# Moving the gate row and the context products later in a fused diffusion layer's projection stage

## The chip, the cores and the metric

The kernel runs on one core of a Trainium2 chip. The metric is the device time of one execution in microseconds (us). A core has a matrix engine (PE, TensorE), three elementwise engines (ACT, ScalarE; DVE, VectorE; POOL, GpSimd) and SP (SyncE), which here does nothing but issue DMA transfers. Each engine carries out its own instructions in order and meets the others through semaphores.

## The reference

One layer on 1024 latent tokens (a 16 by 64 grid) and 256 context tokens, model width 1024, float32. What the change touches is the modulated input, its projection and the gate:

```python
def hybrid_layer(x, ctx, c, c_ctx, w_ada, b_ada, norm_g, w_in, ...):
    shift, scale, gate = adaln(c, w_ada, b_ada)        # silu(c) @ w_ada + b_ada, in three
    shift_c, scale_c, gate_c = adaln(c_ctx, w_ada, b_ada)
    h = rmsnorm(x, norm_g) * (1 + scale[:, None]) + shift[:, None]
    hc = rmsnorm(ctx, norm_g) * (1 + scale_c) + shift_c
    q, k, v, za, u, bg, cg, zc = jnp.split(h @ w_in, SPLIT_POINTS, axis=-1)
    q = rmsnorm(heads(q), q_norm_g)
    k = rmsnorm(heads(k), k_norm_g)
    kc, vc = jnp.split(hc @ w_in[:, D_ATTN:3 * D_ATTN], 2, axis=-1)
    kc = rmsnorm(heads(kc), k_norm_g)
    attn = neighbourhood_attention(q, k, heads(v), kc, vc, rpb) * jax.nn.silu(za)
    conv = gated_short_conv(u, bg, cg, zc, conv_w, conv_b)
    return x + gate[:, None] * (jnp.concatenate([attn, conv], axis=-1) @ w_out)
```

`hc` is what the kernel calls the context's factors; `hc @ w_in[...]` are the context's products; `gate` is the gate row.

## The kernel before, in words

**Four stages.** A first stage (`STEPS`) works out shift and scale, writes the modulated latent input `h`, and already projects the first conv group's three column blocks with it. Its PSUM banks are six accumulators `acc..` and two banks `tr`, in which, among others, the adaLN products lie. Then comes the projection stage, to which the change belongs, then attention (with the remaining projections as filler work for PE), then the output projection.

**The projection stage.** The loop at L1151 runs over steps n = 0 to 34. The 32 token tiles are four head pairs (p = n // 8) by eight tiles of 128 tokens (t = n % 8). In step n, PE projects tile n to q, k and v of pair p (`proj_tile`, L304): 24 matmuls, three for each of eight chunks of 128 rows of the weights, because float32 products are made of a high and a low part. The rest of a tile's work follows in later steps: in step n + 1 ACT squares it and DVE sums (`head_scale`), POOL takes the power -0.5, ACT saves v (`put_v`); in step n + 2 ACT scales it (`rms_normed`: the last read of the tile's bank), and DVE rotates it (`rotated`); at the end of step n + 4, n even, PE transposes tiles n and n + 1 (`turn_qk`), and one step on ACT and DVE split the result and SP stores it. Step t = 4 to 7 of a pair also splits one chunk each of the next pair's weights on ACT and DVE (`chunk_split`), and step t = 0 of the next pair splits the last four, just ahead of its own tile.

**What sets the order.** `strict` (L553) chains the instructions of every engine, SP's transfers included, in the order in which the program writes them. So no engine can pass over an instruction that waits. A PSUM tile of a tag gets its bank when all instructions that touch the tag's earlier tile in that bank are done, those that the program writes further down too. The tags in this stage are O and S (two banks each, tiles `pacc`), U (two banks: `cacc`, `pu`, `pgate`) and C (two banks, transposes).

**The context.** `CONTEXT` (L42) writes the factors `hc` in pairs: DVE scales (`hw`), ACT adds the shift (high part), DVE takes the low part. It is done in step 0 (L1189-1190). In step t = `at` of each pair (L1155: 2, 2, 2, 0), PE makes the context's products of that pair in both U banks (`ctx_products`, L1234); in step `at` + 1 `ctx_sums` and `head_scale` add and square them on ACT and DVE; in step `at` + 2 `normed_ctx` reads them a last time on ACT; in step `at` + 3 `turn_kc` transposes the keys.

**The first conv group.** In steps 5 to 8 PE makes two ticks (six matmuls each) of the projection to the gate path z (`next(group0)`, L1194-1196). Its result lies in tiles `pu` of tag U: one for the first half of the tokens, taken in step 5, one for the second, taken in step 7. The weights for it, `uraw`, are loaded in step 0; ACT casts them to the high parts `uh` at the end of step 0 (`do_acts`, L1228), DVE takes the low parts `ul` in step 1 (`do_dves`).

**The gate row.** `gate.load` (steps 1 to 8) has SP load the 4 MB of its weights in blocks of 512 KB; `gate.add` (steps 2 to 9) multiplies a block and adds it on DVE; `gate.split` (step 11), `gate.sum` (step 13, four matmuls in U banks `pgate`) and a transfer in step 16 (L1175) bring the row to where the output stage needs it. Steps 8, 9, 13, 14, 18, 19, 23 and 24 also add blocks of `w_out` on DVE (`add_blocks`).

Of the kernel before, what the change touches and what calls it, by code (L numbers as in the profile page):

```python
# [23 lines left out]
KT = D // P  # L24
# [3 lines left out]
NPAIR = NH // 2  # L28
# [21 lines left out]
CONTEXT = "Hi0 Hi1 Lo0 Lo1 Hi2 Hi3 Lo2 Lo3 Hi4 Hi5 Lo4 Lo5 Hi6 Hi7 Lo6 Lo7"  # L50
# [5 lines left out]
def body(tc, es, x, xb, xt, cb_, ct, w_mod, w_gate, b_ada, w_grp, w_col, q_g, k_g, bias, w_out, vecs, cst, out):  # L56
# [31 lines left out]
    def mm3(ps, ah, al, bh, bl, first, last):  # L88

        i = pe.matmul(ps, ah, bh, start=first, stop=False)  # L90
        pe.matmul(ps, ah, bl, start=False, stop=False)
        pe.matmul(ps, al, bh, start=False, stop=last)
        return i
# [79 lines left out]
    def chunk_load(col, k):  # L173
        raw = wpp.tile([P, 3, P], F32, name="wr", tag="wr", bufs=5)
        sp.dma_start(raw[:].rearrange("p a n -> p (a n)"), w_grp[NPAIR if col == CU else (col - CQ) // P, k])
        return raw

    def chunk_split(raw):
        raw = raw[:].rearrange("p a b -> p (a b)")
        w = wpp.tile([P, 2, 384], F32R, name="w", tag="w", bufs=12)  # L180
        wh, wl = w[:, 0], w[:, 1]
        act.copy(wh, raw)
        dve.tensor_tensor(wl, raw, wh.bitcast(F32), ALU.subtract)
        return wh, wl, w[:, :, P:384]
# [4 lines left out]
    def head_scale(pp, ps, n):  # L189

        act.activation(sq[:, :n, :HD], by_head(ps[:, :n * HD]), AF.Square, scale=0.125)
        ss = pp.tile([P, 4], F32, name="ss", tag="ss", bufs=7)
        dve.tensor_reduce(ss[:, :n], sq[:, :n], AX.X, ALU.add)
        pool.tensor_tensor(ss[:, :n], ss[:, :n], mhalf[:, :n], ALU.pow)
        return ss
# [10 lines left out]
    def next_vs():  # L206
        vss.append(vss.pop(0))
        return vss[-1]

    def spill_v(p, b, vs):  # L210
        spill(v_d[p][:, :, b:b + 2].rearrange("p s b d -> p s (b d)"), vs.rearrange("p s i d -> p s (i d)"))

    def put_v(vs, i, ps):

        act.copy(vs[:, :, i], ps.rearrange("p (s d) -> p s d", s=2))

    def normed(qn, ps, scale, n):
        for h in range(n):
            cols = slice(h * HD, (h + 1) * HD)
            act.activation(qn[:, cols], ps[:, cols], AF.Identity, scale=scale[:, h:h + 1])  # L220
# [6 lines left out]
    def rms_normed(pp, ps, scale):  # L227

        qn = pp.tile([P, 256], F32, name="qn", tag="qn", bufs=3)
        normed(qn, ps, scale, 4)  # L230
        return qn

    def rotated(pp, rope, qn, t):

        rot = pp.tile([P, 256], F32, name="rot", tag="rot", bufs=3)
        tmp = pp.tile([P, 256], F32, name="rtmp", tag="rtmp", bufs=1)
        for i, to in enumerate((rot, tmp)):
            dve.tensor_tensor(to[:].rearrange("p (k h d) -> p k h d", k=2, h=2),
                              qn[:].rearrange("p (k h d) -> p k h d", k=2, h=2),
                              rope[:, i, t].rearrange("p k (o d) -> p k o d", o=1).broadcast_to([P, 2, 2, HD]),  # L240
                              ALU.mult)
        r4, t4 = (v[:].rearrange("p (h f i) -> p h f i", h=8, f=2) for v in (rot, tmp))
        for f in range(2):
            dve.tensor_tensor(r4[:, :, f], r4[:, :, f], t4[:, :, 1 - f], ALU.add)
        return qn, rot
# [33 lines left out]
    def ctx_sums(pp, acc):  # L279
        for a in acc:  # L280
            other = pp.tile([P, 256], F32, name="rtmp", tag="rtmp")
            act.copy(other, a[:, 256:])
            dve.tensor_tensor(a[:, :256], a[:, :256], other, ALU.add)
# [21 lines left out]
        return put  # L305

    def proj_tile(ch, t):
        ps = bank("pacc", "OOSS"[t % 4])
        for k in range(KT):
            wh, wl = ch[k][:2]  # L310
            mm3(ps[:, :384], hh[k][:, t * P:(t + 1) * P], hl[k][:, t * P:(t + 1) * P], wh, wl, k == 0, k == KT - 1)
        return ps


    def unit_load(col):
        raws = []
        for q in range(2):
            raws.append(uw.tile([P, 4, P], F32, name="uraw", tag="uraw", bufs=2))
            sp.dma_start(raws[q], w_col[col // P, :, 4 * q:4 * q + 4])
        return raws  # L320
# [85 lines left out]
    def z_col(f):  # L406
        return CZA + f * P if f < 4 else CZC + (f - 4) * P
# [342 lines left out]
    def do(steps):  # L750
        for word in steps.split():
            name = word.rstrip("0123456789")
            at = word[len(name):]
            does[name](*([int(at)] if name in ("warm", "fill") else map(int, at)))
# [37 lines left out]
    def bank(name, tag):  # L792
        return (pss if tag == "S" else psm).tile([P, 512], F32, name=name, tag=tag, bufs=2)
# [329 lines left out]
    gate = gate_row()  # L1123
# [5 lines left out]
    def load_blocks(i):  # L1129

        for fs in K_HALVES:
            wsum.append(bmp.tile([P, 3 * 384], F32, name="ws", tag="bt", bufs=2)[:, :D])
            sp.dma_start(wsum[-1], w_out[0, fs[i] * P:(fs[i] + 1) * P])
# [13 lines left out]
    def flush():  # L1147
        while stores:
            stores.pop(0)()

    for n in range(NT + 3):  # L1151


        p, t = divmod(n, NB)
        at = 2 if p < NPAIR - 1 else 0  # L1155
        if t and p + 1 < NPAIR:
            raws.append(chunk_load(CQ + (p + 1) * P, t))
        if n == 0:
            loaded[z_col(4)] = unit_load(z_col(4))
        if n == NT - 8:  # L1160
            loaded[z_col(0)] = unit_load(z_col(0))
        if 1 <= n <= KT:
            gate.load(n - 1)
        if n == NT - 3:
            act.activation(few[:, 5:6], ones, AF.Exp)
        if n == NT - 6:
            heads[0].masks()
            heads[0].load_k()
        if n == NT - 5:
            heads[0].load_q()  # L1170
        flush()
        blocks = divmod(n - 6, 5)
        if 6 <= n < 26 and blocks[1] == 0:
            load_blocks(blocks[0])
        if n == 16:  # L1175
            sp.dma_start(ab[:, :, 0], g_d.rearrange("o (t p) -> p (o t)", p=P))

        if t == 0 and 0 < n < NT:
            nxt += map(chunk_split, raws)
            ch, nxt, raws = nxt, [], []  # L1180
        if t == 0 and p + 1 < NPAIR:
            raws.append(chunk_load(CQ + (p + 1) * P, 0))
        if n == 0:
            next(group0)
        if n == NT - 4:
            next(fill)
        if n < NT:
            tiles[n] = proj_tile(ch, t)
            if n == 0:  # L1189
                do(CONTEXT)  # L1190
        else:
            for _ in range((4, 3, 1)[n - NT]):
                next(fill)
        if 5 <= n < 9:  # L1194
            for _ in range(2):
                next(group0)
        if n == 9:
            for _ in group0:
                pass
        if 0 < n <= NT:  # L1200
            scales[n - 1] = head_scale(pp, tiles[n - 1], 4)
            if n % 2:
                vs = next_vs()
            put_v(vs, (n - 1) % 2, tiles[n - 1][:, 256:384])
            if n % 2 == 0:
                q, r = divmod(n - 1, NB)
                spill_v(q, r - 1, vs)
        if t == at + 1 and n < NT:
            ctx_sums(pp, cacc)
            cscales = [head_scale(pp, a, 2) for a in cacc]  # L1210

        if 1 < n <= NT + 1:
            m, r = n - 2, (n - 2) % NB
            qn = rms_normed(pp, tiles[m], scales.pop(m))
        while waiting:
            waiting.pop(0)()
        if 4 <= t and p + 1 < NPAIR:
            nxt.append(chunk_split(raws.pop(0)))
        if 1 < n <= NT + 1:
            tiles[m] = rotated(pp, rope, qn, r)  # L1220
        if t == at + 2 and n < NT:
            kc = normed_ctx(pp, cacc, cscales)
        do_dves()
        if 6 <= n < 26 and blocks[1] in (2, 3):
            add_blocks(*blocks)
        if 2 <= n < KT + 2:
            gate.add(n - 2)
        do_acts()  # L1228

        if n == KT + 3:  # L1230
            gate.split()
        if n == KT + 5:
            gate.sum()
        if t == at and n < NT:  # L1234
            cacc = ctx_products(ch)
        if n % 2 == 0 and n >= 4:
            waiting.append(turn_qk(pp, (n - 4) // NB, [tiles.pop(n - 4), tiles.pop(n - 3)], (n - 4) % NB))
        if t == at + 3 and n < NT:
            waiting.append(turn_kc(pp, p, *kc))
# [74 lines left out]
    with sbuf("att") as ap, psum("psb") as psb:  # L1314
# [6 lines left out]
        for n in range(len(TICKS)):  # L1321
# [11 lines left out]
            if ready:  # L1333
                p = ready.pop()
# [266 lines left out]
```

## Time and profile before

| what | us |
|---|---|
| median of 3 runs | 588.11 |
| the runs | 587.42 to 588.27 |
| the profiled execution's own time | 587.34 |
| its span, first to last instruction | 585.6 |
| PE busy in the span | 577.2 (99%) |
| DVE busy | 438.6 (75%) |
| ACT busy | 282.0 (48%) |
| POOL busy | 57.4 (10%) |

The span begins with the first instruction. The projection stage's first tile starts on PE at 63.00 us, its last ends at about 241 us. In rows of a timeline, the first two figures are the start and the duration in us; neighbouring instructions of a kind are merged, with their number behind an x; what stands in square brackets is the time for which the engine was idle before, and what ended it. An instruction can start on ACT or DVE while the one before it is still in its last stages, so what counts in a chain is the distance from start to start. The mean granted clock of PE in this execution is 0.999.

### The profile page before, as it was taken

How to read it: one execution, taken by the hardware profiler on the slowest of the kernel's cores; microseconds unless marked ns; L12 is line 12 of the kernel's file. 1: busy time of each engine (PE TensorE's matmuls, PEld its weight loads, DVE VectorE, ACT ScalarE, POOL GpSimd, SP SyncE). 2: the span in 40 equal slices, each digit the busy share in tenths (PEclk: the TensorE clock that was granted, in tenths of full speed). 3: DMA queues.
4: the chain of work that ended last, by engine and by line, in shares of the span. 5: the costliest groups of instructions: out<-in, count | busy, mean ns of one | idle time of the engine just before them, and what ended most of it. 6: DMA issues, size and time to landing. Idle time of an engine off the chain costs nothing.

```text
span 585.6 us, 9903 instructions
## 1 busy us (share of the span) xinstructions
PE 577.2 (99%) x3531; PEld 483.3 (83%) x3532; DVE 438.6 (75%) x890; ACT 282.0 (48%) x653; POOL 57.4 (10%) x82
## 2 busy tenths in 40 slices
PE   8899999999999999999999999999999999999997
PEld 4578999999999999988878787878787867888886
DVE  1578879656846746367998788998979887999952
ACT  5636355336525545433463474466535646643420
POOL 1001033123223232100000000000000001100000
PEclk9999999999999999999999999999999999999999
DMA  8997666845756695686253646564758273773532
GB/s 323 410 415 278 220 229 211 283 166 194 267 189 213 224 341 205 226 297 219 73 209 120 243 140 229 182 216 155 254 187 257 80 263 96 248 252 89 199 125 91
DMA packets 66679, 126.14 MB, mean 215 GB/s; under 512 B 8714, under 2 KB 27650, under 8 KB 64325
## 3 DMA queue, kind: packets, MB, share of 16 engines
q1 hardware_dynamic: 66244, 124.70, 60.8%
q0 software_dynamic: 384, 0.81, 0.6%
q8 instruction: 28, 0.46, 0.3%
q14 instruction: 23, 0.18, 0.1%
HBM read 92.38 MB, written 33.10 MB: 214 GB/s over the span
## 4 chain that ended last, share of the span: by engine, by line
PE 91%; DMA 5%; DVE 2%; ACT 1%; SPq 0%; issue 0%; POOL 0%; DVEq 0%; ACTq 0%
PE pu L71 29%; PE pacc L71 23%; PE pout L71 13%; PE acc L71 5%; PE po L71 5%; PE cacc L71 4%; PE pss L71 3%; DMA xn<-in_xb 3%; PE pc L71 3%; PE pmx L71 2%; PE trA L71 1%; PE tr L71 1%; DMA y_d<-tb 1%; PE ptot L71 1%; PE trB L71 1%; DVE sb L71 0%
## 5 line engine op out<-in xcount | busy, mean ns | idle before, releaser
L71 PE MATMUL pu<-h,uh 128*128 128x512 f32 x544 | 174.4, 402 | 0.0
L71 PE MATMUL pacc<-w,h 128*128 128x384 f32 x768 | 138.5, 337 | 0.0
L71 PEld LDWEIGHTS pacc<-w,h 128*128 128x128 f32 x768 | 132.8, 188 | 0.2
L71 PEld LDWEIGHTS pu<-h,uh 128*128 128x128 f32 x544 | 97.3, 188 | 18.4 <-issue 1.2
L71 PE MATMUL pu<-h,ul 128*128 128x512 f32 x272 | 106.5, 391 | 0.0
L71 PE MATMUL pout<-right,left 128*128 128x512 f32 (+2 forms) x348 | 77.0, 383 | 0.0
L71 PEld LDWEIGHTS pout<-right,left 128*128 128x128 f32 x348 | 64.4, 188 | 12.7
L71 PEld LDWEIGHTS pu<-h,ul 128*128 128x128 f32 x272 | 51.1, 188 | 11.5
L71 POOL TENSOR_TENSOR ss<-ss,few 128x4 f32<-128x4 f32 (+1 forms) x40 | 41.4, 1035 | 127.0 <-DVE ss L71 126.7
L71 ACT COPY sc<-pc 128x512 f32<-128x512 f32 x32 | 18.7, 587 | 44.6 <-PE pc L71 44.6
L71 PE MATMUL acc<-h,w 128*128 128x512 f32 x144 | 35.3, 397 | 1.4 <-ACT h L71 1.4
L71 ACT ACTIVATE sc<-sc 128x512 f32<-128x512 f32 x32 | 20.3, 633 | 33.7 <-DVE sc L71 33.6
L71 ACT ACTIVATE sq<-pacc 128x256 f32<-128x256 f32 x32 | 12.3, 386 | 47.4 <-PE pacc L71 46.7
L71 DVE TENSOR_TENSOR sum<-sum,sb 128x372 f32<-128x372 f32 (+2 forms) x64 | 31.1, 485 | 2.7
L71 PEld LDWEIGHTS acc<-h,w 128*128 128x128 f32 x144 | 26.3, 188 | 7.8 <-ACT h L71 2.1
L71 DVE SCALAR_TENSOR_TENSOR m<-pout,ab,m 128x512 f32<-128x512 f32 (+2 forms) x34 | 22.9, 717 | 13.0 <-PE pout L71 12.9
L71 ACT ACTIVATE qn<-pacc,ss 128x64 f32<-128x64 f32 x128 | 30.0, 330 | 4.8 <-PE trA L71 2.5
L71 DVE TENSOR_TENSOR mx<-mx,sb 128x372 f32<-128x372 f32 (+2 forms) x64 | 30.8, 481 | 1.4
L71 DVE TENSOR_REDUCE ss<-sq 128x4 f32<-128x260 f32 (+1 forms) x40 | 15.7, 393 | 21.5 <-ACT sq L71 21.5
L71 DVE TENSOR_TENSOR ul<-uraw,uh 128x512 fp32r<-128x512 f32 x34 | 23.1, 685 | 10.0 <-ACT uh L71 10.0
L71 DVE TENSOR_TENSOR sb<-pss,bt 128x192 f32<-128x192 f32 (+3 forms) x48 | 27.5, 600 | 2.3 <-PE pss L71 2.2
L71 DVE TENSOR_TENSOR qs<-trA,qs 128x512 fp32r<-128x512 f32 x16 | 11.1, 691 | 21.2 <-ACT qs L71 20.2
(142 smaller groups left out, 862.8 us busy)
## 6 DMA issues: line engine op xcount, KB each, us to landing
uraw<-in_w_col SPq DMA_DIRECT2D x34, 256.0 KB, 3.8
slab<-in_w_mod SPq DMA_DIRECT2D x8, 1024.0 KB, 9.0
q_d<-qs SPq DMA_DIRECT2D x32, 256.0 KB, 4.0
k_s<-k_d SPq DMA_DIRECT2D x8, 1024.0 KB, 6.9
q_s<-q_d SPq DMA_DIRECT2D x16, 512.0 KB, 3.9
wr<-in_w_grp SPq DMA_DIRECT2D x40, 192.0 KB, 5.0
bt<-in_rpb SPq DMA_DIRECT2D x8, 564.0 KB, 6.8
xn<-in_xb SPq DMA_DIRECT2D x8, 512.0 KB
```

What stands on the lines that cost most here:

```text
L71: i = emit(*a, **kw)
```

## The change

Four edits in the projection stage. The gate row's loads, additions, split, sum and last transfer each come eight steps later. The context's factors are written in step 2, after tile 0 is scaled, and no longer in step 0 right behind tile 0's matmuls. The context's products of pair 0 come in step 4 and no longer in step 2 (the other pairs' stay; a fifth entry of the tuple serves the steps beyond the last tile). The tiles with t % 4 of 0 and 1 take the S banks, where the first stage's `tr` tiles lay, and those of 2 and 3 the O banks. Steps 5 to 8 of the first conv group are as they were.

```diff
     def proj_tile(ch, t):
-        ps = bank("pacc", "OOSS"[t % 4])
+        ps = bank("pacc", "SSOO"[t % 4])
...
         p, t = divmod(n, NB)
-        at = 2 if p < NPAIR - 1 else 0
+        at = (4, 2, 2, 0, 0)[p]
...
-        if 1 <= n <= KT:
-            gate.load(n - 1)
+        if 9 <= n <= KT + 8:
+            gate.load(n - 9)
...
-        if n == 16:
+        if n == 24:
             sp.dma_start(ab[:, :, 0], g_d.rearrange("o (t p) -> p (o t)", p=P))
...
             tiles[n] = proj_tile(ch, t)
-            if n == 0:
-                do(CONTEXT)
...
             qn = rms_normed(pp, tiles[m], scales.pop(m))
+        if n == 2:
+            do(CONTEXT)
         while waiting:
             waiting.pop(0)()
...
-        if 2 <= n < KT + 2:
-            gate.add(n - 2)
+        if 10 <= n < KT + 10:
+            gate.add(n - 10)
         do_acts()
 
-        if n == KT + 3:
+        if n == KT + 11:
             gate.split()
-        if n == KT + 5:
+        if n == KT + 13:
             gate.sum()
```

## The prediction, made before the change was run

> **What bounds the kernel now.** I read the busy times first, then the stage that the change touches by windows, then the timelines of PE, ACT and DVE in it. The first view is the table of windows; its columns are the busy time of PE, of PE's weight loads, of DVE, ACT and POOL, then the granted clock.
>
> ```profile
> 63.00:253.00 190.00, 190.00 (x1100) 182.12 (x1099) 125.71 (x304) 89.72 (x318) 46.68 (x51) 1.00 0.68 234
> ```
>
> In the whole projection stage PE is busy for 190.00 of 190.00 us at full clock. So there is no wait of PE that this change could take away, and whatever wait it adds there is added to the end. PE's timeline shows how the stage starts:
>
> ```profile
> 63.00 12.67 PE L71 MATMUL pacc<-w,h 128*128 128x384 f32 x72
> 75.50 5.71 PE L71 MATMUL cacc<-w,hc 128*128 128x512 f32 x32
> 81.05 8.48 PE L71 MATMUL pacc<-w,h 128*128 128x384 f32 x48
> ...
> 89.94 4.43 PE L71 MATMUL pacc<-w,h 128*128 128x384 f32 x24
> 94.22 0.63 PE L71 MATMUL pu<-h,uh 128*128 128x512 f32 x2
> ```
>
> Three tiles take 75.50 - 63.00 = 12.50 us, so 4.17 each; the context's products take 81.05 - 75.50 = 5.55; between tile 4's end at 81.05 + 8.33 = 89.38 and 89.94 stand six transposes, 0.56; tile 5 takes 4.28; then the conv group takes its first `pu` bank.
>
> **The change, part by part: who holds the U banks in step 5.** With `at` = 4, PE does tiles 0 to 4 (63.00 + 5 x 4.17 = 83.85), the products (to 89.40), the transposes (89.96) and tile 5 (94.24), and then comes `pu`, as before the change. But the products now hold both U banks, and their last reader is `normed_ctx`, in step `at` + 2 = 6. In ACT's order that stands behind the squaring of tile 5, which PE finishes only at 94.24. So PE must wait at `pu`, and behind `pu` everything of PE is queued. Before, step `at` + 2 was step 4, and the banks were free in time. This wait is certain in the code; its length is ACT's and DVE's backlog. To lay that out I need the rows of the stage's start, of SP, then DVE and POOL, then ACT:
>
> ```profile
> 70.80 0.82 SPq L71 DMA_DIRECT2D uraw<-in_w_col  x2
> ```
> ```profile
> uraw<-in_w_col SPq DMA_DIRECT2D x34, 256.0 KB, 3.8
> ```
> ```profile
> 70.47 0.87 DVE L71 SCALAR_TENSOR_TENSOR hw<-xc,ab,rs 128x256 f32<-128x256 f32 x2
> ...
> 77.10 0.88 DVE L71 SCALAR_TENSOR_TENSOR hc<-hw,ab,hc 128x256 fp32r<-128x256 f32 x2 [0.18 <-ACT hc L71]
> 78.88 0.42 DVE L71 TENSOR_REDUCE ss<-sq 128x4 f32<-128x260 f32 x1 [0.89 <-ACT sq L71]
> 79.22 1.28 DVE L71 TENSOR_TENSOR ul<-uraw,uh 128x512 fp32r<-128x512 f32 x2
> ```
> ```profile
> 81.79 0.42 DVE L71 TENSOR_TENSOR rot<-qn,rope 128x256 f32<-128x256 f32 x1 [0.95 <-ACT qn L71]
> ...
> 83.00 1.41 DVE L71 SCALAR_TENSOR_TENSOR gacc<-gs,c,gacc 128x512 f32<-128x512 f32 x2
> ```
> ```profile
> 79.38 1.41 POOL L71 TENSOR_TENSOR ss<-ss,few 128x4 f32<-128x4 f32 x1 [8.95 <-DVE ss L71]
> ```
> ```profile
> 77.38 1.13 ACT L71 CAST uh<-uraw 128x512 fp32r<-128x512 f32 x2
> 78.41 0.37 ACT L71 ACTIVATE sq<-pacc 128x256 f32<-128x256 f32 x1
> ...
> 80.83 0.93 ACT L71 ACTIVATE qn<-pacc,ss 128x64 f32<-128x64 f32 x4 [0.89 <-POOL ss L71]
> ```
>
> Before, the factors (7.51 us, from 70.47 to 77.98 on DVE) ran while `uraw` was on its way, and the cast of `uraw` found its data there. Now the cast is what ACT comes to first, right behind the first stage, and the factors are behind it in step 2. SP issues `uraw` at 70.80 and about 71.2 as before (nothing ahead of it moves); with the median of 3.8 us it lands at 75.0 or, behind the rope table issued just before it, later. I take 75.8 for the second half; the ends are 75.0 and 77.4, where the cast stood without a wait. So ACT, and with it DVE, stands idle until 75.8 while tiles 0 to 2 are already done. From there:
>
> Tile 0 is squared at 76.3 (half of 1.13 on), its sum is there at 77.1 (0.37 + 0.42), its power at 78.1 to 78.5 (POOL has 1.03 to 1.41), and ACT has scaled it at about 79.3. DVE does the sum, `ul` and the sum of tile 1 (0.33 + 1.20 + 0.33 from 76.7) to 78.6, then the factors, 7.5, to 86.2. Then rotation of tile 0 (81.79 to 83.00: 1.2), sum of tile 2 (0.33), rotation of tile 1 (1.2), sum of tile 3 (0.33): 89.3. There it waits for ACT's first chunk cast, which stands behind the scaling of tile 2 (sum at 87.8, power 1.0, scaling 0.8, cast 0.55: 90.2), then low part of the chunk 0.5, rotation of tile 2 1.2, sum of tile 4 0.33: at 92.3 DVE comes to the first of the two context sums, which PE had ready at 89.4. From the second copy of a sum on, the same work stands in ACT's rows of pair 1:
>
> ```profile
> 134.03 0.37 ACT L71 COPY rtmp<-cacc 128x256 f32<-128x256 f32 x1 [0.56 <-PE trA L71]
> ...
> 136.78 1.20 ACT L71 CAST gp<-gacc 128x512 fp32r<-128x512 f32 x2
> 138.29 0.38 ACT L71 ACTIVATE sq<-pacc 128x256 f32<-128x256 f32 x1 [0.32 <-PE pacc L71]
> ...
> 139.51 0.55 ACT L71 CAST w<-wr 128x384 fp32r<-128x384 f32 x1
> 139.91 0.57 ACT L71 ACTIVATE kn<-cacc,ss 128x64 f32<-128x64 f32 x2
> 140.32 0.32 ACT L71 COPY vs<-cacc 128x128 f32<-128x128 f32 x1
> ```
>
> The second copy starts at 92.3 + 0.43 (a sum of this width, like the 0.42 of the rotation's) + 0.05 = 92.8. To the end of the transposes' casts it is 136.78 - 134.03 = 2.75; `gp` isn't there in step 5 now, but a chunk cast is (0.40); tile 5's squaring to the chunk cast of step 6 is 139.51 - 138.29 = 1.22; from there to the release of the first bank 140.64 - 139.51 = 1.13. Together 92.8 + 5.5 = 98.3. PE waits from 94.2 to 98.3: **4.1 us**. Bounds: were ACT not behind at all, only tile 5's squaring to the release would follow PE (0.2 + 2.35, so 2.6); with `uraw` at 77.4 it is 1.6 more, 5.7.
>
> **The gate row.** Its additions leave steps 2 to 9, where DVE's time was hidden, and where DVE's backlog above is already counted without them. They come in steps 10 to 17, a pair of 1.33 us each (83.00, 1.41 long, less the overlap). In steps 10 and 11 DVE idles for the context's products and takes them up; in 11 `gate.split` (1.2 us) goes as well; from step 12 on they add up until step 16, in which the last four weight chunks of pair 2 must be split just ahead of tile 16. DVE's rows of steps 13 to 16, and PE's:
>
> ```profile
> 144.33 0.69 DVE L71 TENSOR_TENSOR qs<-trA,qs 128x512 fp32r<-128x512 f32 x1 [0.96 <-ACT qs L71]
> ...
> 146.93 1.41 DVE L71 TENSOR_TENSOR ws<-ws 128x512 f32<-128x512 f32 x2
> ...
> 150.31 0.42 DVE L71 TENSOR_TENSOR ks<-trC,ks 128x256 fp32r<-128x256 f32 x1 [0.70 <-ACT ks L71]
> ...
> 152.40 1.41 DVE L71 TENSOR_TENSOR ws<-ws 128x512 f32<-128x512 f32 x2
> ...
> 154.51 0.69 DVE L71 TENSOR_TENSOR qs<-trA,qs 128x512 fp32r<-128x512 f32 x1 [0.36 <-ACT qs L71]
> ...
> 157.11 1.96 DVE L71 TENSOR_TENSOR w<-wr,w 128x384 fp32r<-128x384 f32 x4
> ```
> ```profile
> 147.10 1.09 PE L71 MATMUL pgate<-gp,oner 128*1 128x512 f32 x4
> 148.03 0.38 PE L71 MATMUL trC<-ci,kn 128*128 128x128 f32 x2
> ...
> 153.01 8.60 PE L71 MATMUL pacc<-w,h 128*128 128x384 f32 x48
> ```
>
> All in before's times: step 13 starts its transposes' part at 144.33 and ends its `w_out` part at 148.26; with the pair 149.6. Step 14: sum 0.33, then 150.31 to 153.73 (3.42), pair: 154.7. Step 15: sum 0.33, 154.51 to 157.11 (2.60), pair: 158.9. The first of the four chunks is split 0.55 later, at 159.45. PE comes to tile 16 at 153.01 + 4.27 = 157.28, less the 0.93 of `pgate`, which now is in step 21: 156.35; it needs that chunk's low part at its fourteenth matmul, 13 x 0.174 later, at 158.6. Wait: **0.8 us**; the further chunks (0.49 each) keep ahead of PE (0.52 each). Before, the slack there was 1.9. Ends: 0, if DVE keeps up, and 2.1, if step 12's pair isn't absorbed either. The eight loads move on SP past the chunk loads and stores of pair 1; each waits for a buffer that DVE frees two steps ahead of its use; a late one would lengthen the 0.8, within its upper end. `pgate` costs PE its 0.93 in either place; step 24's transfer has nobody waiting until the output stage.
>
> **Parts that cost nothing.** The S banks' last reader is ACT's copy of the context's row, the last of twelve `tr` tiles and so in the second bank:
>
> ```profile
> 63.30 0.38 ACT L71 COPY rs<-tr 128x256 f32<-128x256 f32 x1
> ```
>
> It is done at 63.7, and the bank is needed for tile 1 at 67.17; were it the first bank, 0.7. Tile 4 needs tile 0's bank at 79.68, tile 0 is scaled at 79.3: hidden by 0.4, up to 1.0 if `uraw` is late. The factors' last pair is there at 86.2, and PE comes to it at 83.85 + 6 x 0.69 = 88.0. The transposes at 89.4 need tile 1 rotated at 89.0.
>
> **The sum.** 4.1 + 0.8 = 4.9. Against the profiled execution's own time 587.34 + 4.9 = 592.2; the median of the runs lies 0.77 above that execution, so 593.0 is what I give.
>
> **Rivals.** One: the wait lets PE's clock fall. The rows of PE's start price that:
>
> ```profile
> 1.52 2.74 PE L71 MATMUL acc<-warm 128*128 128x512 bf16 x6 [1.52 <-POOL warm L71]
> ...
> 4.48 3.20 PE L71 MATMUL acc<-warm 128*128 128x512 bf16 x14
> ```
> ```profile
> PE acc L71 <- POOL warm L71: 1.5, 1, 1.5
> ```
>
> The same matmul takes 2.74 / 6 = 0.46 us first and 3.20 / 14 = 0.23 later: for about 2.9 us PE ran at half rate and lost some 1.4. Losing that once or twice behind the wait gives 594.4 to 595.8, middle 595.1. Against it: 4.1 us is short, but the longest wait in PE's whole list is the 1.5 us at the very start, so nothing in this trace shows either way; I give it 0.20. [...]
>
> Two, not slower: `pu` finds a U bank in time. The place is step 5, and the point is whether ACT's last read of the first context accumulator ends before 94.2. Then only the gate row's 0.8 is left: 588.9, within what can be told from no change. For it: before the change the banks were never waited for. Against it: the program order puts the read behind tile 5's end. 0.12.
>
> Three, faster: DVE's relief in steps 2 to 9 and the earlier squaring of tile 0 pay. Against it: PE's 190.00 of 190.00; nothing there can be won, and more than 1.2 us would be needed. 0.03. A last 0.03 is for further waits behind a late `uraw`, above 596.
>
> **How the numbers follow.** My forecast has 0.62; with its bounds alone it spans 588.11 + 2.6 = 590.7 to 588.11 + 7.8 = 595.9. The range 590.6 to 596.0 leaves out rival two, rival three and the last case, 0.18. About 0.2% (1.2 us) is what a measurement of this kernel can tell from no change: faster 0.03, same 0.12, slower 0.85.
>
> **What would show it.** Right: PE's waits name `pu` <- ACT `vs` (or `kn`) with about 4 us near 94, and `pacc` <- DVE `w` with about 0.8 us at tile 16 near 161 to 163; ACT idles some 10 us ahead of `uh`, for `uraw`; all else on PE is shifted by the sum. Wrong: PE without a gap at 94, a gap at another step of the first eight, matmuls of 0.35 us behind the gap (rival one), or a sum of PE's gaps that isn't the difference of the times.

## The result and the profile after

The changed kernel takes 596.13 us (median of 4 runs: 595.63, 595.74, 596.52, 599.0) beside 587.87 us for the kernel before on the same chip (4 runs, 587.42 to 588.27). The ratio is 1.0156, with a 95% interval of 1.0142 to 1.0169: slower. (Ratios here are worked out from the executions of both kernels, not from the two medians, whose quotient is 1.0141.) The forecast was 593.0 with 590.6 to 596.0 around it, so the direction is right and the time lies 0.13 us above the range. The profiled execution took 595.63 us with a span of 593.9, beside 587.34 and 585.6 before: 8.3 us more in both. One execution of e9 below, which took 1488.66 us, was a disturbed one and is left out of its ratio.

PE's list of waits in the changed kernel (columns: total, times, longest, all in us) has three entries of the projection stage that the list before did not have:

```profile
PE pu L71 <- ACT vs L71: 4.5, 1, 4.5
...
PE pacc L71 <- DVE w L71: 1.1, 1, 1.1
...
PE pacc L71 <- ACT qn L71: 0.2, 1, 0.2
```

The first two are the waits that the prediction named, at the places that it named. PE's timeline shows them with what stands around them:

```profile
80.29 4.45 PE L71 MATMUL pacc<-w,h 128*128 128x384 f32 x24 [0.24 <-ACT qn L71]
84.58 5.71 PE L71 MATMUL cacc<-w,hc 128*128 128x512 f32 x32
...
90.70 4.44 PE L71 MATMUL pacc<-w,h 128*128 128x384 f32 x24
99.66 0.73 PE L71 MATMUL pu<-h,uh 128*128 128x512 f32 x2 [4.52 <-ACT vs L71]
...
100.58 1.05 PE L71 MATMUL pu<-h,uh 128*128 128x512 f32 x2
101.43 0.63 PE L71 MATMUL pu<-h,ul 128*128 128x512 f32 x1
101.86 1.05 PE L71 MATMUL pu<-h,uh 128*128 128x512 f32 x2
...
159.80 6.08 PE L71 MATMUL pacc<-w,h 128*128 128x384 f32 x34
166.98 2.21 PE L71 MATMUL pacc<-w,h 128*128 128x384 f32 x11 [1.09 <-DVE w L71]
```

Tile 5 ends at 90.70 + 4.44 = 95.14, and `pu` starts 4.52 us later. Look then at the `pu` rows behind the wait: from the pair at 100.58 to the single product at 101.43 it is 0.85 us, so 0.43 for each matmul, and from the single to the next pair another 0.43. At full clock the same matmul takes 0.23 (experiment e8 below shows it in this very place). The windows of the changed kernel around the wait (length, busy time of PE, weight loads, DVE, ACT, POOL, then the granted clock, the DMA share and GB/s) show the cause:

```profile
95.00:99.60 4.60, 0.14 (x1) 0.00 (x0) 3.21 (x10) 4.50 (x20) 1.36 (x2) 1.00 0.06 11
99.60:100.30 0.70, 0.64 (x3) 0.55 (x4) 0.70 (x3) 0.59 (x4) 0.49 (x1) 1.00 0.88 321
100.30:103.70 3.40, 3.40 (x10) 2.62 (x9) 1.33 (x4) 0.00 (x0) 1.68 (x3) 0.50 0.97 277
103.70:106.00 2.30, 2.30 (x14) 2.21 (x13) 0.00 (x0) 0.00 (x0) 0.00 (x0) 0.99 1.00 376
```

During the wait ACT is busy for 4.50 of 4.60 us: it is ACT's queue that PE waits for. PE resumes at 99.66 at a granted clock of 1.00, and only 0.64 us later the clock drops to 0.50, for 3.4 us (100.30 to 103.70), and then returns to 0.99. That is the prediction's first rival.

From the first tile's start to the last tile's start PE's timeline gives 181.92 us, beside 173.61 before. Each part of these 8.31 us is a distance from start to start across one place, less the same distance before the change. Such a part is 0.1 to 0.3 us longer than the wait itself, because the last matmul ahead of a wait runs out before the wait begins (0.34 us at 79.71, ahead of tile 4's, where matmuls follow each other at 0.17), and the first ones behind it follow more slowly (the first two `pu` take 0.57 us, 99.66 to 100.23, beside 0.46 before, 94.22 to 94.68):

| part | predicted | measured in this profile |
|---|---|---|
| U banks in step 5 | 4.1 (2.6 to 5.7) | 4.7 |
| gate row, at tile 16 | 0.8 (0 to 2.1) | 1.4 |
| tile 4's bank | 0 | 0.5 |
| clock at half | 0 (rival: 1.4 to 2.8) | 1.7 |
| sum | 4.9 | 8.3 |

The clock's part is the first `pu` group, 4.45 us from its start to the next tile's, beside 2.76 before. About 0.1 of it belongs to the restart: in e7, where the clock stayed up behind a wait, the group takes 2.85.

### The profile page after: what moved, and what is told of

Read it like the earlier page. It is cut to its first block, busy times and chain, and to the rows that moved or that the text cites. A ratio compares the mean times of both kernels' runs of the same rounds, so it can differ in the third digit from the quotient of the medians.

```text
span 593.9 us, 9897 instructions
## 1 busy us (share of the span) xinstructions
PE 579.8 (98%) x3531; PEld 484.3 (82%) x3532; DVE 438.3 (74%) x890; ACT 282.5 (48%) x653; POOL 57.3 (10%) x82
## 4 chain that ended last, share of the span: by engine, by line
PE 76%; DVE 9%; DMA 7%; ACT 4%; issue 2%; POOL 1%; SPq 0%; DVEq 0%; ACTq 0%; POOLq 0%
PE pu L71 29%; PE pacc L71 14%; PE pout L71 13%; PE po L71 5%; PE pss L71 3%; PE cacc L71 3%; PE pc L71 2%; PE pmx L71 2%; DMA xh<-in_xt 2%; PE acc L71 1%; DMA wr<-in_w_grp 1%; DMA xn<-in_xb 1%; DMA y_d<-tb 1%; DVE gacc L71 1%; DVE hw L71 1%
## 5 line engine op out<-in xcount | busy, mean ns | idle before, releaser
L71 DVE TENSOR_TENSOR sb<-sb,mg 128x744 f32<-128x744 f32 (+2 forms) x32 | 26.7, 833 | 0.0
```

Source lines behind the costliest of these rows:

```text
L71: i = emit(*a, **kw)
```

## The experiments

My theory after this comparison: four separate costs that add up, each with a cause of its own. The rivals were that the new order of the banks has a share in it, that the whole gate term comes from the queue of SP and not from DVE's additions, and that the clock falls only behind a window without any work of PE, as long as the half-clock stretch measured above, 3.4 us.

**e1: the gate row alone.** The kernel before, with only the gate row's steps changed:

```diff
-        if 1 <= n <= KT:
-            gate.load(n - 1)
+        if 9 <= n <= KT + 8:
+            gate.load(n - 9)
...
-        if n == 16:
+        if n == 24:
...
-        if 2 <= n < KT + 2:
-            gate.add(n - 2)
+        if 10 <= n < KT + 10:
+            gate.add(n - 10)
...
-        if n == KT + 3:
+        if n == KT + 11:
             gate.split()
-        if n == KT + 5:
+        if n == KT + 13:
             gate.sum()
```

> Only the gate row's edits (eight steps later); factors, products and banks as before. My theory (DVE reaches the last four weight chunks of pair 2 late, because three pairs of additions stand ahead of them): one wait of PE, pacc <- DVE w, of 0.8 to 1.3 us at tile 16, nothing else: 588.9 to 589.2. Rival (the gate's 4 MB now crowd the transfers of pair 1's chunks): PE or ACT waits that name a transfer, over several tiles, 2 us or more. Rival (all of the loss hangs on the U banks): no wait at tile 16 and the time of before, 587.9.

Measured: 588.69 us, beside 587.17 for the kernel before; ratio 1.0021 (1.0011 to 1.0032). The one new wait of PE in the stage, and rows of SP, ACT and DVE ahead of it:

```profile
PE pacc L71 <- DVE w L71: 1.1, 1, 1.1
```
```profile
149.33 0.99 SPq L71 DMA_DIRECT2D gs<-in_w_gate  x2
150.38 1.43 SPq L71 DMA_DIRECT2D q_d<-qs  x2
151.85 0.45 SPq L71 DMA_DIRECT2D k_d<-ks  x1
```
```profile
155.69 0.37 ACT L71 CAST ks<-trB 128x256 fp32r<-128x256 f32 x1 [1.86 <-DMA k_d<-ks]
```
```profile
153.54 1.41 DVE L71 SCALAR_TENSOR_TENSOR gacc<-gs,c,gacc 128x512 f32<-128x512 f32 x2
...
156.10 0.42 DVE L71 TENSOR_TENSOR ks<-trB,ks 128x256 fp32r<-128x256 f32 x1 [0.21 <-ACT ks L71]
```

And the row of the same store in the kernel before:

```profile
147.17 0.47 SPq L71 DMA_DIRECT2D k_d<-ks  x1
```

Read them in order. The gate's load waits in SP's queue until DVE has freed its buffer (between 140 and 165 us SP waits for DVE's `gacc` four times, 2.8 us at the longest), and the stores of Q and K stand behind it. So `k_d` is issued at 151.85; before it was at 147.17. ACT's next cast into the buffer `ks` must wait for that store, 1.86 us, and DVE 0.21 us for ACT. The time is 1.5 us above that of the kernel before, about what was expected, and PE's stage is longer by the same 1.4. The gate term thus stands alone, at the size that it has in the changed kernel (1.1 of pure wait in both), and it does not depend on the U banks.

**e2: the banks alone.**

```diff
-        ps = bank("pacc", "OOSS"[t % 4])
+        ps = bank("pacc", "SSOO"[t % 4])
```

> Only the order of the banks (S first). My theory: none of the banks is needed before it is free, so 587.9 within 0.3 and no wait of PE in the stage. Rival (the 0.25 us that PE waited at tile 4 in the changed kernel come from the banks' order): a wait at tile 0, 1 or 4, 588.1 to 588.6.

Measured: 587.6 us, ratio 1.0008 (0.9999 to 1.0017). The window of the projection stage:

```profile
63.40:253.40 190.00, 190.00 (x1100) 182.10 (x1099) 125.73 (x304) 89.91 (x318) 46.70 (x51) 1.00 0.67 233
```

PE is busy throughout, so the first tiles' banks cost nothing.

**e3: the change, with the gate row two steps later instead of eight.** The loads are in steps 3 to 10 and the additions in 4 to 11. (At their old place the loads' buffers are still those that the context's factors need.)

```diff
-        if 9 <= n <= KT + 8:
-            gate.load(n - 9)
+        if 3 <= n <= KT + 2:
+            gate.load(n - 3)
...
-        if 10 <= n < KT + 10:
-            gate.add(n - 10)
+        if 4 <= n < KT + 4:
+            gate.add(n - 4)
```

with the row's split, sum and transfer brought forward by six steps as well.

> The changed kernel with the gate row two steps later than before the change, not eight (at its old place its buffers are the ones that the factors of step 2 still need). My theory: no wait at tile 16, since the last addition is in step 11; the wait at pu in step 5 is there and longer than 4.5 us, 5.5 to 7, since DVE has additions in step 4 and 5 again; the clock falls behind it as in the changed kernel, 1.7 us or more: in all 595 to 597. Rival (the moved gate row is the main loss): 590 or less.

Measured: 596.24 us, ratio 1.016 (1.0145 to 1.0174). PE's waits, two windows, and two rows of DVE:

```profile
PE pu L71 <- ACT vs L71: 5.6, 1, 5.6
...
PE pacc L71 <- ACT qn L71: 0.3, 1, 0.3
```
```profile
94.60:98.60 4.00, 0.10 (x1) 0.00 (x0) 2.17 (x6) 3.42 (x14) 2.10 (x3) 1.00 0.47 144
98.60:105.40 6.80, 5.10 (x12) 4.04 (x13) 6.21 (x15) 2.23 (x11) 3.43 (x3) 0.50 0.61 196
```

```profile
92.51 1.41 DVE L71 SCALAR_TENSOR_TENSOR gacc<-gs,c,gacc 128x512 f32<-128x512 f32 x2
...
94.17 0.42 DVE L71 TENSOR_TENSOR cacc<-cacc,rtmp 128x256 f32<-128x256 f32 x1
```

The wait at tile 16 is gone and the one at `pu` is 1.1 us longer, because the additions stand in DVE's queue again while it is behind: the last rows show a pair of them just ahead of the first context sum. Here PE's idle time reaches into the half-clock stretch, which lasts twice as long: 6.8 us, of which PE works for 5.10, so that about half of that, 2.6 us, is lost. A gain of 1.4 at tile 16 is paid back at `pu` and in the clock.

**e4: the change, with the conv group's products one step later.**

```diff
-        if 5 <= n < 9:
+        if 6 <= n < 10:
             for _ in range(2):
                 next(group0)
-        if n == 9:
+        if n == 10:
             for _ in group0:
```

> The changed kernel with the conv group's ticks in steps 6 to 9, no longer 5 to 8. My theory (pu comes for a U bank one step before the context's products are read): PE does tile 6 where it waited, the wait at pu falls to 0 to 0.5 us, the clock stays at full rate, and only tile 16's 1.1 us, tile 4's 0.25 us and that rest are left: 589.3 to 589.8. Rival (ACT's late start, not the bank, holds PE): a wait of 3 us or more elsewhere in steps 4 to 7, 592 or more.

Measured: 591.81 us, ratio 1.0082 (1.0068 to 1.0096); granted clock 1.00 in the profiled execution, which took 590.87. PE's waits:

```profile
PE pacc L71 <- DVE w L71: 2.0, 1, 2.0
...
PE pacc L71 <- ACT qn L71: 0.5, 1, 0.5
...
PE pu L71 <- ACT vs L71: 0.4, 1, 0.4
```

One step is enough for the U banks: 4.5 us of wait become 0.4, and the profiled execution keeps its clock. One of the five timed runs does not (593.66 us, mean clock 0.997); which wait brought that down is not recorded. The median is 2.0 us above the upper end of its expectation. Larger than reckoned were the wait at tile 16, 2.0 instead of 1.1 us, and tile 4's, 0.5 instead of 0.25; besides, the median lies 0.9 above the profiled execution. Rows of SP and ACT at tile 16:

```profile
153.34 0.49 SPq L71 DMA_DIRECT2D k_d<-ks  x1
```
```profile
157.83 0.38 ACT L71 CAST ks<-trB 128x256 fp32r<-128x256 f32 x1 [2.77 <-DMA k_d<-ks]
```

From the store's issue to the start of the cast that waits for it, it is 4.49 us here, 3.84 in e1 and 3.62 in the changed kernel. The store's issue lies 6.9 us ahead of the point at which PE has to wait, in the changed kernel 7.0, so it is the store itself that took longer. Why it did is not shown.

**e5 to e8: how much idleness lowers the clock.** Matmuls of zeros are added to the changed kernel in front of `pu`, in the bank that the next tile takes and overwrites; nothing of the computation is left out. Four kernels differ only in their number, 4, 8, 12 and 20:

```diff
-        ps = bank("pacc", "SSOO"[t % 4])
+        ps = early_bank.pop() if early_bank else bank("pacc", "SSOO"[t % 4])
...
+    early_bank = []
...
+        if n == 5:
+            early_bank.append(bank("pacc", "SSOO"[(t + 1) % 4]))
+            for _ in range(4):
+                pe.matmul(early_bank[0][:].rearrange("p (a n) -> p a n", a=4), zeros,
+                          zeros[:].rearrange("p (o n) -> p o n", o=1).broadcast_to([P, 4, P]), start=True, stop=True)
         if 5 <= n < 9:
```

> The changed kernel with 4 matmuls of zeros (0.22 us each, into the bank that tile 6 overwrites next) in front of the pu of step 5: additional work, nothing left out. They take the first 0.9 us of the 4.5 that PE waits, so it idles 3.6 us; the wait's end stays. Theory A (the clock falls when a fixed window of about 3.4 us is mostly idle): it falls in most runs, 1.7 us as in the changed kernel, 595.5 to 596.5. Theory B (only a window without any activity counts): 3.6 us hold such a window in few runs: clock full in most, 594.0 to 594.5.

> The same with 8 matmuls, 1.8 us of the wait: PE idles about 2.7 us. Theory A: the clock falls in some runs or none (2.7 of a window of 3.4 is 80% idle, as much as the window behind which it fell in the changed kernel): 594.1 to 596. Theory B: never, 594.1 to 594.5, mean clock as before the change.

> The same with 12 matmuls, 2.6 us: PE idles about 1.9 us. Both theories: the clock does not fall, 594.1 to 594.5: the changed kernel less 1.7 us or more.

> The same with 20 matmuls, 4.3 us: PE idles under 0.4 us. My theory (wait and clock are two losses): the matmuls behind pu run at 0.23 us and not 0.43, the time is 1.7 us or more below the changed kernel's, 594.0 to 594.5, and the rest of the difference, 6.2 us, stays. Rival (the slow matmuls behind the wait have another cause, such as their weights coming late): still 0.43 us each, and the changed kernel's time.

| zeros | us | ratio (95%) | idle ahead of `pu`, profiled, us | clock in the profile | mean clock of each timed run |
|---|---|---|---|---|---|
| 4 | 596.58 | 1.0161 (1.0146 to 1.0177) | 3.7 | half for at least 3.3 us | 0.997, 0.997, 0.997, 0.994 |
| 8 | 595.40 | 1.0139 (1.0124 to 1.0154) | 2.8 | half for 3.4 us | 0.997, 0.996, 1.0, 0.997 |
| 12 | 594.91 | 1.0143 (1.0118 to 1.0168) | 1.9 | full | 1.0, 0.996, 1.0, 0.997 |
| 20 | 595.00 | 1.0130 (1.0115 to 1.0145) | 0.2 | full | 0.999 to 1.0 |

One stretch of 3.4 us at half rate takes 1.7 of 595 us off the mean, which gives 0.997, as in the profiled execution of the changed kernel. The windows of e6 (8 zeros) show such a stretch behind a shorter wait:

```profile
96.10:99.50 3.40, 0.64 (x3) 0.10 (x1) 2.90 (x8) 3.40 (x15) 0.27 (x1) 1.00 0.09 14
99.50:102.90 3.40, 3.38 (x8) 2.70 (x9) 1.99 (x6) 0.55 (x3) 2.17 (x3) 0.50 0.94 276
```

In the 3.4 us ahead of the drop PE worked for 0.64 us, so the window was idle for only about 80% of its length, and the clock fell all the same. PE's whole idle stretch there is 2.78 us, so no window of 3.4 us can have been wholly idle. The rival that asks for one is out. In the changed kernel it was the same: the 3.4 us ahead of the drop at 100.3 hold 2.76 us of idleness (96.9 to 99.66) and 0.64 of work. With 12 zeros the profiled execution kept its clock; two of the four timed runs did not, which I had not expected. Their waits were not recorded, so how much idleness is enough stays open. With 8 zeros it fell in three timed runs (mean clocks 0.996 and 0.997) and one kept it (1.0).

In e8 no stretch is lost; PE's timeline behind the zeros, one of PE's waits, and ACT's cast of `uraw`:

```profile
96.10 4.49 PE L71 MATMUL pacc<-zeros 128*128 128x512 bf16 x20
100.78 0.72 PE L71 MATMUL pu<-h,uh 128*128 128x512 f32 x2 [0.20 <-ACT vs L71]
...
101.57 0.62 PE L71 MATMUL pu<-h,uh 128*128 128x512 f32 x2
```
```profile
PE pacc L71 <- ACT qn L71: 1.2, 1, 1.2
```
```profile
76.93 1.18 ACT L71 CAST uh<-uraw 128x512 fp32r<-128x512 f32 x2 [11.16 <-DMA uraw<-in_w_col]
```

There a `pu` matmul takes 0.23 us, not 0.43. Still the profiled execution is only 0.7 us below that of the changed kernel (594.93 beside 595.63). In it the wait for tile 4's bank was 1.2 us instead of 0.2, because the cast of `uraw` began at 76.93, 1.1 later than in the changed kernel (SP had issued the load 0.5 later, and from the issue to the cast it was 0.6 longer); that took back 1.0 of the 1.7.

**e9 and e10: the gate term, by DVE and by SP.** Both are e1 with one more edit. In e9 the pair of additions of step 15 is moved into step 16, and so behind the split of the four chunks; in e10 the gate's loads stand behind the stores in SP's queue.

```diff
-        if 10 <= n < KT + 10:
-            gate.add(n - 10)
+        for kt in (5, 6) if n == 16 else (n - 10,) if 10 <= n < KT + 10 and n != 15 else ():
+            gate.add(kt)
         do_acts()
```

> The gate row alone eight steps later, as in e1, but the addition of step 15 is done in step 16, behind the split of the four weight chunks. My theory (the additions in steps 13 to 15 make DVE late for those splits): DVE comes to them 1.3 us earlier, so of the 1.1 us nothing or at most 0.2 us is left, and the time is before's, 587.1 to 587.5. Rival (the chunks' data or ACT's casts come late): the wait stays at 0.8 us or more, 588.2 to 588.7.

```diff
-        if 9 <= n <= KT + 8:
-            gate.load(n - 9)
...
         flush()
+        if 9 <= n <= KT + 8:
+            gate.load(n - 9)
```

> The gate row alone eight steps later, as in e1, but SP issues each step's stores ahead of its gate loads. In e1 ACT waited 1.9 us in step 15 for the store of an earlier k tile, which stood on SP behind a gate load that waits for DVE, and DVE then waited 0.2 us for ACT. Theory A (DVE's own additions make the wait at tile 16): the wait falls by that 0.2 us only, to 0.8 to 0.9. Theory B (the queue on SP makes it): it is gone, 587.1 to 587.4.

e9 takes 587.67 us, ratio 1.0001 (0.9992 to 1.0009): the gate term is gone. (Its profile is that of the execution of 1488.66 us, so PE's waits in e9 are not shown, and this rests on the times of the other ten.) e10 takes 588.60 us, ratio 1.0018 (1.001 to 1.0027), with this line among PE's waits:

```profile
PE pacc L71 <- DVE w L71: 1.0, 2, 0.7
```

ACT waits for no store any more, and PE's wait at tile 16 is 0.7 us instead of 1.1 (the other 0.3 is one at tile 0, for a chunk of the stage's start). So neither theory of e10 holds alone: 0.4 of the wait hangs on the queue of SP, and 0.7 is there without it. All of it needs the additions ahead of the split, as e9's time shows. The times do not separate e10 from e1, whose intervals overlap; the split of 0.7 and 0.4 rests on one profile of each.

**e11: the change, with the cast of `uraw` behind the factors.**

```diff
-        do_acts()
+        if n > 1:
+            do_acts()
```

> The changed kernel with the casts of uraw on ACT behind the factors (end of step 2), no longer at the end of step 0. My theory (the cast's wait for its transfer holds ACT until 75.8, and that backlog is what stretches the wait at pu): ACT works from 67 on, no wait at tile 4, the wait at pu falls from 4.5 to about 2.6 us, which is what the order of the loop alone costs; tile 16's stays at 0.8 to 1.2. With e6 and e7 2.6 us of idleness let the clock fall in some runs and not in others: 590.9 to 591.5 without, 1.7 more with. Rival (the backlog is the factors' own 7.5 us): the wait stays at 4 us or more, 594 to 596.

Measured: 595.18 us (592.53 to 596.26), ratio 1.0123 (1.0102 to 1.0144). PE's waits in the profiled execution, the one of 592.53:

```profile
PE pu L71 <- ACT vs L71: 2.4, 1, 2.4
...
PE pacc L71 <- DVE w L71: 2.2, 2, 1.1
```

The wait at `pu` came down to 2.4, as expected, and tile 4's is gone; the second line now holds 1.1 at tile 16 and 1.1 at tile 0, where ACT had waited 1.6 us for a transfer of the stage's first weights. The wait at tile 0 puts this execution about 1 us above what was expected of a run at full clock, and the median is higher still: the mean clocks of the six runs are 1.0, 0.994, 0.997, 0.994, 0.994 and 0.996. The clock fell in five of six, though the one execution whose wait is on record, 2.4 us, kept it. The cast's place is the reason for ACT's late start; taking it away removes about 2 us of the wait, not all of it, and the clock still falls in most runs.

**e12: the change, with all of these undone.** The conv products one step later (e4), the cast late (e11), the additions behind the split (e9) and the loads behind the stores (e10), on top of the changed kernel:

> The changed kernel with the conv group's ticks in steps 6 to 9 (e4), the casts of uraw behind the factors (e11), the addition of step 15 behind the split (e9) and the stores ahead of the gate loads (e10); the four edits of the change all stand. My theory: PE then has no wait over 0.7 us in the stage, the clock stays up, and the time is that of before within 0.2% (586.5 to 588.3): the change as such costs nothing and wins nothing. Rival (something else in the change costs time, such as the moved transfers): 589.5 or more.

Measured: 587.61 us, ratio 1.0003 (0.9994 to 1.0011). The window of the stage:

```profile
63.00:253.00 190.00, 189.87 (x1098) 181.71 (x1097) 125.45 (x304) 90.20 (x319) 46.21 (x51) 1.00 0.68 233
```

All edits of the change still stand in this kernel. With the waits gone it takes the time of the kernel before: within the interval of about 0.1%, nothing else in the change costs anything, and nothing in it gains anything. PE is busy for 189.87 of 190.00 us there, so a further edit of this kind has 0.13 us left to win in the stage.

## Why the prediction was right, and where it failed

**The U banks: right in mechanism, 0.6 us too small.** The prediction placed PE's wait at `pu` behind ACT's read of the first context accumulator, and its backlog behind the late `uraw`. ACT's rows in the changed kernel, then DVE's:

```profile
75.81 1.16 ACT L71 CAST uh<-uraw 128x512 fp32r<-128x512 f32 x2 [10.53 <-DMA uraw<-in_w_col]
76.88 0.38 ACT L71 ACTIVATE sq<-pacc 128x256 f32<-128x256 f32 x1
...
94.04 0.37 ACT L71 COPY rtmp<-cacc 128x256 f32<-128x256 f32 x1 [0.56 <-DVE cacc L71]
...
97.20 0.44 ACT L71 ACTIVATE sq<-pacc 128x256 f32<-128x256 f32 x1
98.82 0.63 ACT L71 ACTIVATE kn<-cacc,ss 128x64 f32<-128x64 f32 x2
99.23 0.38 ACT L71 COPY vs<-cacc 128x128 f32<-128x128 f32 x1
```
```profile
79.24 0.87 DVE L71 SCALAR_TENSOR_TENSOR hw<-xc,ab,rs 128x256 f32<-128x256 f32 x2
...
86.25 0.88 DVE L71 SCALAR_TENSOR_TENSOR hc<-hw,ab,hc 128x256 fp32r<-128x256 f32 x2 [0.18 <-ACT hc L71]
93.52 0.43 DVE L71 TENSOR_TENSOR cacc<-cacc,rtmp 128x256 f32<-128x256 f32 x1 [0.16 <-ACT rtmp L71]
```

The cast starts at 75.81, which looks like the 75.8 of the working. But that was meant for the second half of `uraw`, with the first half's cast already done. In the trace each half lands 4.8 us after its issue, not 3.8, and 75.81 is the start of the first half's cast. So tile 0 is squared behind both halves, at 76.88 and not 76.3. The factors start 0.6 later for it, at 79.24, the first context sum comes at 93.52 instead of 92.3, and the first bank is free at 99.23 + 0.38 = 99.6 instead of 98.3. From the second copy (94.04) to the release it is 5.6 us, against 5.5 from the rows of pair 1: borrowing those rows worked. Of these 1.3 us PE itself came 0.9 later to the wait (95.14 beside 94.2, for tile 4's wait and the stage's later start), so the pure wait is 4.5 instead of 4.1, and with the 0.2 behind it the term is 4.7.

**The gate row: right in place, 0.6 us too small.** The DVE queue was costed, and by e10 it alone makes 0.7 of pure wait, near the 0.8 given. What was left out is SP's queue: the text considered that a gate load could itself be late, and not that the stores behind it on SP are delayed while it waits for its buffer. In e1's rows this is the store at 151.85, ACT's 1.86 and DVE's 0.21; without it the wait is 0.4 shorter. The last 0.3 of the 1.4 passed just ahead of and behind the wait.

**Tile 4: the step "hidden by 0.4" failed.** It took tile 0's scaling at 79.3 and PE's arrival at 79.68. In the changed kernel PE waited 0.24 us and lost 0.5 in all. The margin was as thin as the error of the chain that it was worked out from; the prediction's own "up to 1.0 if `uraw` is late" was the right hint, and e8's 1.2 us shows it.

**The clock: put at nothing, and the largest single miss.** The sum of 4.9 has no term for it. The text called a wait of 4.1 us short and gave rival one 0.20; both were the author's estimate, as the trace before shows no longer wait than 1.5 us. The clock fell in all four timed runs (mean clocks 0.997, 0.997, 0.990 and 0.994), and in e6 it fell behind 3.4 us of which four fifths (2.76) were idle. The rival's price was near (1.4 us for one stretch; measured 1.7, as for 3.4 us at half rate), its chance was not. That price came from PE's start, where the granted clock on record reads 1.00 (1.52 to 4.20 us): the half rate was read there from the matmuls' 0.46 us alone.

The three other terms were together 1.7 us too small, as much as the clock's. Either shortfall alone would have left the median at about 594.4, within the range; the two together put it above, and above the 594.4 to 595.8 of rival one as well. In two of the four runs the mean clock (0.990 and 0.994) points to more than one stretch, by an estimate from the 0.997 of one; where is not recorded.

**Rivals two and three** are out: `pu` did not find its bank (4.52 us), and nothing was won elsewhere (e12's ratio 1.0003). **The parts at nothing** other than tile 4 hold: the banks' order by e2, and the factors, the transposes and `pgate`'s new place because PE's list of waits in the changed kernel has no entry for them and e12 finds no further cost.

## What to carry to other kernels

When work moves later, look at who reads its accumulators last and what is queued for that reader, in program order, against the next tile that takes the bank; here one step's distance, in which the reader stood behind the tile just finished, cost a wait of 2.4 us without the reader's late start (e11) and of 4.5 with it, and putting the bank's next user one step later left 0.4. A wait of PE is to be priced together with the clock behind it: here the clock fell to 0.50 in every profiled execution that waited 2.8 us or more (2.8, 3.7, 4.5 and 5.6 in e6, e5, the changed kernel and e3), and the mean clock was 0.994 to 0.997 in some timed runs of kernels whose profile shows 1.9 to 2.4. When a load with a buffer to wait for enters an in-order queue, price the stores behind it and the buffers that those stores release: in e1 the store of K was issued 4.7 us later than before (151.85 beside 147.17), and ACT waited 1.86 us for it.

## What the runs showed of the hardware

The granted clock fell to 0.50 behind 3.4 us that were about four fifths idle (2.76 us in the changed kernel, 2.76 in e6); in e6 PE's whole idle stretch was 2.78 us, so no 3.4 us there were idle throughout. In these profiles the drop is not tied to PE's restart: in the changed kernel PE restarted at 99.66 and the clock fell at 100.3, in e6 the two came together (99.52 and 99.5), and in e3 the clock fell at 98.6, ahead of the restart at 100.30. The half rate lasted 3.4 us in the changed kernel and in e6 and at least 3.3 in e5 (100.60 to 103.90), and 6.8 in e3, where PE was still idle from 98.6 to 100.30.

Kernels whose longest wait in the projection stage of the profile is about 2 us (e4, e7, e11: 2.0, 1.9 and 2.4) kept a clock of 1.00 in that profile and show a lower mean in some timed runs: 0.997 in one of five, 0.996 and 0.997 in two of four, 0.994 to 0.997 in five of six. Where the clock falls, the times spread: 592.53 to 596.26 for e11 and 595.63 to 599.0 for the changed kernel, beside 2.0 and 0.9 us for the kernel before in the same two comparisons.
